# One hybrid mLSTM and attention encoder layer on one core: the seven-product weights on ScalarE's queue, their buffers in changing roles, and the merged projection's operands in six half-heads

## The chip, the core and the metric

The kernel runs on one core of a Trainium2 chip. Five engines work beside each other, each through its own list of instructions in order: PE (TensorE, matmul), DVE (VectorE), ACT (ScalarE), POOL (GpSimd) and SP (SyncE, which in this kernel issues the DMAs). The metric is the device time of one execution in microseconds. Three runs of the kernel before gave 1942.12, 1938.83 and 1942.77 us; their median is 1942.12 us.

## The reference

Two groups of 512 tokens go through the same layer with the same weights, all in 32-bit floating point. Cut to what matters here:

```python
h = rmsnorm(x, g_mix)
qk, v, o, gates, c_q, c_kv, k_r, gm = split(h @ w_in)
hm = mlstm(q, k, v, gates)                   # both directions, 4 heads of 256 columns
hm = rmsnorm(hm, g_mhead)
y_m = (sigmoid(o) * hm) @ w_mo               # 1024 x 1024
y_a = mla_attention(...) @ w_ao              # 8 heads of 128, w_ao 1024 x 1024
x = x + (sigmoid(gm_m) * y_m + sigmoid(gm_a) * y_a) @ w_out
h2 = rmsnorm(x, g_ffn)
x = x + (silu(h2 @ w_gate) * (h2 @ w_up)) @ w_down
x = x + sigmoid(x @ w_ple_gate) * (p @ w_ple)
return rmsnorm(x, g_final)
```

## The kernel before

**Products.** Every 32-bit product is made of three passes: an operand is split into a high part (`xh`, `whi`, written by a copy on ACT) and a low part (`xl`, `wlo`, written by a subtraction on DVE, `lo_of`), and high times high, low times high and high times low are added in PSUM. One pass is one MATMUL of 128x128 by 128x512. So each 128x512 tile that enters a matmul costs one ACT cast and one DVE subtraction.

**Seven products.** The large weight matrices (`w_mo`, `w_ao`, gate, up and down) are taken in 2x2 blocks, two row halves by the two token groups, with seven block products in place of eight. An object `Seven` holds one such 2x2 block of a weight: two 512 KB loads (`srcs[0]` with a11 and a12, `srcs[1]` with a21 and a22) go into two staging buffers `wst`, one from the pool WP and one from the pool WX. `weights(name)` gives the weights of one of the products P1, P2, P7, P6, P5, Q4, P3, in part by sums on POOL (`s3` for P7, then in place in a11, a21, a12), and `wsplit` splits them into a `wp` tile. P1, P2, P6 and P3 read the first buffer, P5 and Q4 the second, and P7 the sum `s3` of a11 and a21. The data operands of the seven products are held by an object `Ops`: from four tiles a, b, c, d for each k of four it makes the seven combinations (P1 = a, P2 = c, P7 = b - d, and so on, `part`), and `need` splits each.

**Chain.** `chain()` runs a list of `Seven`s with the products of neighbours interleaved (P6, next P1, P5, next P2, Q4, next P7, P3), and `outputs()` copies results from the PSUM bank b1 to a tile `u` on ACT and combines banks on DVE. The FFN's gate and up run as such `Seven`s from about 1186 us to 1586 us, its down from there to 1826 us, `w_mo` and `w_ao` from about 872 us to 1050 us.

**Attention.** From about 575 us to 872 us the loop over `hd` runs eight heads, each for two groups (sixteen half-heads). At head 7 it opens the pool X2, and there `hops.need` builds the data operands P1, P2 and P7 of the merged mLSTM projection (`w_mo`). `hraw` loads one tile of the mLSTM's result from `hzd` in DRAM and scales it in place by the per-row factors `hg` with an ACTIVATE. `hzd` is written by `mlstm_finish`, as (`to` + 1) times the transposed state.

**Order.** A scheduler lays the instructions of each engine in order from its own timeline model, except in sections between `pinned[0] = True` and `False`, whose order is the code's. The section around the embedding (`emb`) and the tail (from `finish(0, ...)` to the end) are pinned. All instructions of an engine pass through the wrapper `Engine` and carry the line of its call, L77; the DMAs carry their own lines (L849 the loads of `Seven`, L164 the other weights, L773 and L938 loads of activations, L982 the stores of z1d).

**Embedding and tail.** `emb` makes the products with `w_ple`, whose four splits are appended to `wple` when the first of their two columns comes up. At the end the last group is normalised in two halves of its tokens: `sums` adds squares over partitions by matmuls (`ssc`), `inv` makes the reciprocal root, `spread3` broadcasts it (`rbc`), and `finish` multiplies the output columns (`o`) and stores them.

Of the kernel before, what the change touches and what calls it, by code (L numbers as in the profile page):

```python
# [20 lines left out]
KD = D // P  # L21
# [41 lines left out]
def encoder_kernel(ctx: ExitStack, tc: tile.TileContext, a):  # L63
# [3 lines left out]
    class Engine:  # L67
# [5 lines left out]
        def __getattr__(self, name):  # L73
            f = getattr(self.e, name)

            def call(*args, **kw):
                r = f(*args, **kw)  # L77
                if pinned[0]:
                    tc.keep_in_program_order(r)
                return r  # L80

            return call

    V, S, E, GP = (Engine(e) for e in (nc.vector, nc.scalar, nc.tensor, nc.gpsimd))

# [376 lines left out]
    def mlstm_proj(hd):  # L462
# [59 lines left out]
        for c in range(2):  # L522
            w = w8(f"o{2 * hd + c}")
            for g in range(G):
                to[g][c] = hproj(w, g, M1("to", "to"))
                S.activation(out=to[g][c], in_=to[g][c], func=AF.Tanh, scale=0.5)
        mst[hd] = (sts, va, to)

    def mlstm_chain(hd, g):
# [67 lines left out]
        for c in range(2):  # L597
            tp = bank("ht")
            for i in range(NB):
                E.transpose(tp[:, i * P : (i + 1) * P], hm[:, i, c * P : (c + 1) * P], ident)  # L600
            zt = EV("ch", "hz")
            V.scalar_tensor_tensor(out=zt, in0=to[g][c], scalar=1.0, in1=tp, op0=ALU.add, op1=ALU.mult)
            nc.sync.dma_start(hzd[g][2 * hd + c], zt)
# [180 lines left out]
    class Ops:  # L784
# [12 lines left out]
        def part(self, name, k):  # L797
# [3 lines left out]
            if name == "P7":  # L801
                t = self.t[k] = self.tmp()
                add(out=t, in0=self.get("b", k), in1=self.get("d", k), op=ALU.subtract)
            elif name == "P6":
                t = self.t[k]
                add(out=t, in0=t, in1=self.get("a", k), op=ALU.subtract)
            elif name == "P5":
                t = self.get("a", k)
                add(out=t, in0=t, in1=self.get("b", k), op=ALU.subtract)
            else:  # L810
                t = self.t[k]
                add(out=t, in0=t, in1=self.get("c", k), op=ALU.add)
            return t
# [12 lines left out]
    wpn = [0]  # L826
# [14 lines left out]
    class Seven:  # L841


        def __init__(self, srcs, kh, ops, out):
            n = kh * P
            st = []
            for sl, src in zip((WP, WX), srcs):
                t = sl("wst", "wst", F32, (P, 1024))
                nc.sync.dma_start(t[:, : 2 * n], src)  # L849
                st += [t[:, 0:n], t[:, n : 2 * n]]  # L850
            self.st, self.n, self.kh, self.ops, self.out = st, n, kh, ops, out
            self.bk = {}
# [39 lines left out]
    def chain(quads, head=False, look=4):  # L892
# [10 lines left out]
        made = {}  # L903
        for at, (q, n) in enumerate(order):
            for i, m in order[at : at + look + 1]:
                quads[i][0].need(m)
            for i, m in order[at : at + 2]:
                if i not in made:
                    made[i] = quads[i][1]()
# [31 lines left out]

    def hraw(g, k):
        t = load(hzd[g][k], X2, "x")
        S.activation(out=t, in_=t, func=AF.Copy, scale=hg[:, k : k + 1])
        return t

    tmps = [(H, "rs"), (H, "rs"), (EV, "bk"), (EV, "bk")]
    hops = Ops(hraw, lambda: (lambda s: s[0](s[1], "t"))(tmps.pop(0)), lambda n: V if n == "P7" else GP)
# [5 lines left out]
    for hd in range(AH):  # L954
        if hd < AH - 1:
            wa = weight(a["wa"][hd + 1])
        else:
            QL.close()
            X2 = Slots("X2", "right", x=16)
            for n in ("P1", "P2", "P7"):  # L960
                hops.need(n)
        for g in range(G):
            attn(hd, g, ops[g])
            if hd < AH - 1:
                ops[g] = attn_proj(hd + 1, g, wa)
        for _ in range(BULK[2 + hd]):
# [109 lines left out]
    def emb(n):  # L1076
        for _ in range(n):
            c, g = todo.pop(0)
            if c // 2 == len(wple):
# [209 lines left out]
    finish(1, [0, 1, 2, 3], 0, H0)  # L1289
    embed(KD - 1, 1, bk[3], toks[1], bps[1])  # L1290
    sums(1, H0, H0)
    inv(1, H0)
    rs_ = rs2[1]
    spread3(1, H0, H0)
    rs2[1], rs_ = rs_, rs2[1]
    finish(1, [4, 5, 6, 7], 0, H0)
    rs2[1] = rs_
# [11 lines left out]
LEAD = 2  # L1309
LATN = (3, 0)  # L1310
# [94 lines left out]
```

## Time and profile before

| what | value |
|---|---|
| runs | 1942.12, 1938.83, 1942.77 us, median 1942.12 |
| profiled execution | 1939.74 us |
| its span, first to last instruction | 1938.0 us |
| mean granted PE clock | 0.981 |
| PE | 1861.9 us busy, x8836 |
| PE weight loads | 1542.6 us busy |
| DVE | 1260.3 us busy, x2135 |
| ACT | 874.7 us busy, x1711 |
| POOL | 474.4 us busy, x349 |
| DMA | 203.40 MB, mean 105 GB/s |

The profile shows one execution. Its time lies 2.38 us below the median of the runs, and 1.74 us of it lie outside the span. A busy PE means that a matmul is in flight; matmuls overlap (one lasts about 390 ns, and the next begins some 230 ns after it), so a short wait shows less idle time than it costs. In the views of stretches the columns are: the stretch and its length, then the busy time and number of instructions of PE, PE's weight loads, DVE, ACT and POOL, then the granted PE clock (1.00 is full), the DMA engines' busy share and the GB/s moved. In the chain of work that ended last each line is a start, a duration and what ran.

### The profile page before, as it was taken

The page shows a single profiled execution, that of the slowest core. Times are in us where ns is not written, and L with a number is a line of the kernel's source. Part 1 is how long each engine was busy: PE and PEld are TensorE (multiplying, and loading weights), DVE is VectorE, ACT ScalarE, POOL GpSimd, SP SyncE. Part 2 cuts the span into 40 slices and gives each one's busy share as a digit, 9 for nine tenths or more (in the row PEclk, how much of TensorE's full clock was granted, in tenths as well). Part 3 has the DMA queues.
Part 4 walks back from the last instruction along what each step waited for, and adds up shares of the span by engine and source line. Part 5 has one row for each costly group of instructions (what it writes and reads, how often), then busy time and mean ns, then how long its engine had stood idle before and what let it go on. Part 6 is the DMA issues. An engine that isn't in the chain of part 4 may idle for free. (4 is left out here: it accounts for less than half of the span.)

```text
span 1938.0 us, 24531 instructions
## 1 busy us (share of the span) xinstructions
PE 1861.9 (96%) x8836; PEld 1542.6 (80%) x8836; DVE 1260.3 (65%) x2135; ACT 874.7 (45%) x1711; POOL 474.4 (24%) x349
## 2 busy tenths in 40 slices
PE   7999999999999999979899989999999999999997
PEld 6888898988888888758777867777887777788886
DVE  7657575746455676878996667445444458778757
ACT  5245454535354566784533435233333344434442
POOL 3000000100000001234630014565466654232100
PEclk9999999999999999989999989999999999999998
DMA  4110112012262122137554331233223346534232
GB/s 161 50 44 33 55 35 64 34 60 82 82 202 90 55 74 73 53 115 239 163 200 153 109 114 66 87 111 106 94 97 102 115 135 218 163 120 142 87 125 87
DMA packets 95578, 203.40 MB, mean 105 GB/s; under 512 B 10400, under 2 KB 21024, under 8 KB 95456
## 3 DMA queue, kind: packets, MB, share of 16 engines
q1 hardware_dynamic: 95456, 201.83, 31.2%
q8 instruction: 69, 1.13, 0.2%
q14 instruction: 53, 0.43, 0.1%
HBM read 147.69 MB, written 54.10 MB: 104 GB/s over the span
## 5 line engine op out<-in xcount | busy, mean ns | idle before, releaser
L77 PE MATMUL b<-xh,wp 128*128 128x512 f32 x2296 | 723.4, 396 | 17.9 <-ACT wp L77 8.3
L77 PEld LDWEIGHTS b<-xh,wp 128*128 128x128 f32 x2296 | 434.5, 190 | 124.4 <-ACT wp L77 11.7
L77 PE MATMUL b<-xl,wp 128*128 128x512 f32 x1148 | 452.4, 394 | 5.9 <-DVE xl L77 5.7
L77 DVE TENSOR_TENSOR wp<-wst,wp 128x512 fp32r<-128x512 f32 (+1 forms) x284 | 271.9, 964 | 108.8 <-ACT wp L77 108.0
L77 ACT CAST wp<-wst 128x512 fp32r<-128x512 f32 (+1 forms) x284 | 171.0, 611 | 345.4 <-PE b L77 228.1
L77 PEld LDWEIGHTS b<-xl,wp 128*128 128x128 f32 x1148 | 217.8, 190 | 54.3 <-DVE xl L77 7.6
L77 PE MATMUL mm<-hh,whi 128*128 128x512 f32 x592 | 233.1, 394 | 7.2 <-ACT whi L77 7.0
L77 PE MATMUL mm<-hh,wlo 128*128 128x512 f32 x592 | 232.4, 394 | 2.2 <-DVE wlo L77 2.2
L77 PE MATMUL mm<-hl,whi 128*128 128x512 f32 x592 | 233.0, 394 | 1.1 <-DVE hl L77 1.1
L77 POOL TENSOR_TENSOR s<-wst,wst 128x512 f32<-128x512 f32 (+1 forms) x42 | 61.6, 1466 | 449.5 <-DMA wst<-w 323.4
L77 PEld LDWEIGHTS mm<-hh,whi 128*128 128x128 f32 x592 | 112.2, 190 | 30.6 <-ACT whi L77 7.0
L77 POOL TENSOR_TENSOR wst<-wst 128x512 f32<-128x512 f32 (+1 forms) x84 | 125.7, 1496 | 35.3 <-DVE wp L77 30.7
L77 PEld LDWEIGHTS mm<-hh,wlo 128*128 128x128 f32 x592 | 112.1, 189 | 26.1 <-DVE wlo L77 3.4
L77 PEld LDWEIGHTS mm<-hl,whi 128*128 128x128 f32 x592 | 112.1, 189 | 25.5 <-DVE hl L77 2.3
L77 DVE TENSOR_TENSOR u<-b,u 128x512 f32<-128x512 f32 x90 | 61.3, 687 | 107.6 <-PE b L77 82.7
L77 ACT CAST whi<-wst 128x1024 fp32r<-128x1024 f32 (+1 forms) x71 | 73.1, 1029 | 110.4 <-PE mm L77 77.6
L77 DVE TENSOR_TENSOR wlo<-wst,whi 128x1024 fp32r<-128x1024 f32 (+1 forms) x71 | 86.0, 1211 | 28.7 <-ACT whi L77 28.3
L77 POOL TENSOR_TENSOR vnl<-avt,vnh 128x512 fp32r<-128x512 f32 x16 | 21.5, 1345 | 317.6 <-ACT vnh L77 284.6
L77 DVE TENSOR_TENSOR xl<-ld,xh 128x512 fp32r<-128x512 f32 x109 | 88.7, 846 | 8.1 <-ACT xh L77 7.8
L77 PE MATMUL mm<-xh,wp 128*128 128x512 f32 (+1 forms) x288 | 81.7, 368 | 0.0
L77 ACT COPY u<-b 128x512 f32<-128x512 f32 x90 | 50.9, 586 | 66.6 <-PE b L77 65.6
L77 DVE TENSOR_TENSOR x<-x,b 128x512 f32<-128x512 f32 x84 | 56.9, 682 | 32.8 <-PE b L77 32.4
(269 smaller groups left out, 3379.4 us busy)
## 6 DMA issues: line engine op xcount, KB each, us to landing
wst<-w SPq DMA_DIRECT2D x135, 512.0 KB
ld<-actd SPq DMA_DIRECT2D x77, 256.0 KB
actd<-t SPq DMA_DIRECT2D x44, 256.0 KB
actd<-sg SPq DMA_DIRECT2D x33, 256.0 KB
x<-x SPq DMA_DIRECT2D x32, 256.0 KB
wst<-wd SPq DMA_DIRECT2D x16, 512.0 KB
hzd<-hz SPq DMA_DIRECT2D x16, 256.0 KB
tmd<-tg SPq DMA_DIRECT2D x16, 256.0 KB
```

The costliest lines, as they stand in the source:

```text
L77: r = f(*args, **kw)
```

## The change

1. `Seven` loads its weights with `S.dma_start`, so 84 loads leave SP's list and stand in ACT's. The pools of its two buffers change roles every two `Seven`s (`wsn`): the first load takes the pool WP in two of four, WX in the other two. The first buffer of a `Seven` thus follows the second buffer of the `Seven` two before, which is last read for Q4, and no longer that one's first buffer, which is last read for P3, the last product.
2. The operands P1, P2, P7 and P6 of the merged mLSTM projection are made in single (name, k) units behind the half-heads named in `HOPS`: three behind each half of heads 4 and 5, two behind each half of head 6. They load through four staging buffers. At head 7 the four tiles are loaded again into X2 for P5, Q4 and P3, so `hzd` is read 32 times (16 before, 256 KB each). Q4's operand is made of c - a - d by two POOL operations. The factor `hg` moves into `mlstm_proj`: an ACTIVATE (Identity, scale and bias `hc`) on `to` there, 16 in all, in place of the 16 scalings of the loads; `mlstm_finish` multiplies with `tensor_tensor`.
3. `emb` makes each `wple` split one ahead of its use.
4. In the tail `finish(1, ...)` of the first token half is split: two columns before the last `embed`, two behind it, two more between `inv` and `spread3`, two behind. The last `embed` runs with `keep=True`: it adds no squares on DVE, and `ssc` takes four more matmuls.
5. `Engine` gives back the plain method outside pinned sections. This changes only the line numbers in the profile: there instructions carry their own lines (L843 the cast and L152 the subtraction of a split, L855 the loads of `Seven`, L929 the copies to `u`).

The core of the diff:

```diff
                 S.activation(out=to[g][c], in_=to[g][c], func=AF.Tanh, scale=0.5)
+                hc = hg[:, 2 * hd + c : 2 * hd + c + 1]
+                S.activation(out=to[g][c], in_=to[g][c], func=AF.Identity, scale=hc, bias=hc)
...
-            V.scalar_tensor_tensor(out=zt, in0=to[g][c], scalar=1.0, in1=tp, op0=ALU.add, op1=ALU.mult)
+            V.tensor_tensor(out=zt, in0=to[g][c], in1=tp, op=ALU.mult)
...
-            else:
+            elif k in self.t:
                 t = self.t[k]
                 add(out=t, in0=t, in1=self.get("c", k), op=ALU.add)
+            else:
+                t = self.get("c", k)
+                add(out=t, in0=t, in1=self.get("a", k), op=ALU.subtract)
+                add(out=t, in0=t, in1=self.get("d", k), op=ALU.subtract)
...
-            for sl, src in zip((WP, WX), srcs):
+            for sl, src in zip((WP, WX) if wsn[0] % 4 < 2 else (WX, WP), srcs):
                 t = sl("wst", "wst", F32, (P, 1024))
-                nc.sync.dma_start(t[:, : 2 * n], src)
+                S.dma_start(t[:, : 2 * n], src)
                 st += [t[:, 0:n], t[:, n : 2 * n]]
+            wsn[0] += 1
...
+    stage = [(H, "rs"), (H, "rs"), (EV, "bk"), (EV, "bk")]
+    raws = [0]
+
     def hraw(g, k):
-        t = load(hzd[g][k], X2, "x")
-        S.activation(out=t, in_=t, func=AF.Copy, scale=hg[:, k : k + 1])
-        return t
...
+        raws[0] += 1
+        return load(hzd[g][k], *stage[raws[0] % 4])
...
+    units = [(n, [k]) for k in range(4) for n in ("P1", "P2", "P7", "P6")]
...
             X2 = Slots("X2", "right", x=16)
-            for n in ("P1", "P2", "P7"):
-                hops.need(n)
+            hops.r, hops.t = {}, {}
+            hops.raw = lambda g, k: load(hzd[g][k], X2, "x")
         for g in range(G):
             attn(hd, g, ops[g])
             if hd < AH - 1:
                 ops[g] = attn_proj(hd + 1, g, wa)
+            for _ in range(HOPS.get((hd, g), 0)):
+                hops.need(*units.pop(0))
...
-            if c // 2 == len(wple):
+            while len(wple) < min(4, c // 2 + 2):
...
-    finish(1, [0, 1, 2, 3], 0, H0)
-    embed(KD - 1, 1, bk[3], toks[1], bps[1])
+    first = rs2[1]
+    finish(1, [0, 1], 0, H0)
+    embed(KD - 1, 1, bk[3], toks[1], bps[1], True)
+    finish(1, [2, 3], 0, H0)
     sums(1, H0, H0)
     inv(1, H0)
-    rs_ = rs2[1]
+    finish(1, [4, 5], 0, H0)
     spread3(1, H0, H0)
...
-    finish(1, [4, 5, 6, 7], 0, H0)
+    finish(1, [6, 7], 0, H0)
...
+HOPS = {(4, 0): 3, (4, 1): 3, (5, 0): 3, (5, 1): 3, (6, 0): 2, (6, 1): 2}
```

**ACT in the FFN.** ACT's list at the change from one gate and up `Seven` to the next, before (`wp` are split weights, `s3` and `wst` their sources, `b1` a PSUM bank, `u` its copy):

```order
L77 CAST wp_2297_12504<-wst_2263_12313 128x512
L77 CAST wp_2302_12542<-wst_2263_12313 128x512
L77 CAST wp_2305_12563<-s3_2304_12560 128x512
L77 CAST wp_2307_12580<-wst_2262_12311 128x512
L77 COPY u_2293_12484<-b1_2267_12336 128x512
L77 COPY u_2296_12502<-b1_2295_12489 128x512
L77 CAST wp_2313_12619<-wst_2309_12597 128x512
L77 CAST wp_2311_12602<-wst_2290_12464 128x512
L77 COPY u_2298_12519<-b1_2267_12336 128x512
L77 CAST wp_2318_12656<-wst_2309_12597 128x512
```

The same place with the change (the `wst` tiles of the new loads are the first and the second buffer of the `Seven` after the next):

```order
L843 CAST wp_2309_12536<-wst_2275_12345 128x512
L843 CAST wp_2314_12574<-wst_2275_12345 128x512
L855 DMA wst_2321_12629<-w8 128x1024
L843 CAST wp_2317_12595<-s3_2316_12592 128x512
L843 CAST wp_2319_12612<-wst_2274_12343 128x512
L855 DMA wst_2322_12631<-w8 128x1024
L929 COPY u_2305_12516<-b1_2279_12368 128x512
L929 COPY u_2308_12534<-b1_2307_12521 128x512
L843 CAST wp_2325_12651<-wst_2321_12629 128x512
L843 CAST wp_2323_12634<-wst_2302_12496 128x512
L929 COPY u_2310_12551<-b1_2279_12368 128x512
L843 CAST wp_2330_12688<-wst_2321_12629 128x512
```

Two loads now stand in ACT's list behind the casts of Q4 and of P3 and ahead of the two copies to `u`. The first takes the buffer that Q4 has just read, the second the buffer that P3 has just read.

**DVE in the attention.** DVE's list beside the low part `qnl` of the queries for the second half of head 4, before (`wlo` is a low part of attention weights, `sc` are scores, `mx` their row values, `p` probabilities, `qnl` a low part of queries):

```order
L77 TENSOR_TENSOR qs1_1185_7163<-rp_1182_7154,qs1_1185_7163 64x512
L77 TENSOR_TENSOR wlo_1211_7328<-wst_1209_7324,whi_1210_7326 128x768
L77 TENSOR_REDUCE mx_1215_7338<-sc_1214_7332 128x1
L77 TENSOR_TENSOR qnl_1188_7177<-pj_1186_7168,qnh_1187_7175 128x512
L77 TENSOR_SCALAR mx_1215_7338<-mx_1215_7338 128x1
L77 TENSOR_REDUCE mx_1219_7358<-sc_1218_7352 128x1
L77 RECIPROCAL mx_1215_7338<-mx_1215_7338 128x1
L77 TENSOR_SCALAR mx_1219_7358<-mx_1219_7358 128x1
```

The same place with the change:

```order
L724 TENSOR_TENSOR qs1_1185_7179<-rp_1182_7170,qs1_1185_7179 64x512
L152 TENSOR_TENSOR xl_1243_7476<-ld_1241_7472,xh_1242_7474 128x512
L152 TENSOR_TENSOR wlo_1211_7344<-wst_1209_7340,whi_1210_7342 128x768
L748 TENSOR_REDUCE mx_1215_7354<-sc_1214_7348 128x1
L152 TENSOR_TENSOR xl_1246_7482<-ld_1244_7478,xh_1245_7480 128x512
L152 TENSOR_TENSOR qnl_1188_7193<-pj_1186_7184,qnh_1187_7191 128x512
L749 TENSOR_SCALAR mx_1215_7354<-mx_1215_7354 128x1
L748 TENSOR_REDUCE mx_1219_7374<-sc_1218_7368 128x1
L749 TENSOR_SCALAR mx_1219_7374<-mx_1219_7374 128x1
L752 RECIPROCAL mx_1215_7354<-mx_1215_7354 128x1
L805 TENSOR_TENSOR ld_1247_7484<-ld_1247_7484,ld_1248_7486 128x512
L752 RECIPROCAL mx_1219_7374<-mx_1219_7374 128x1
```

Two subtractions `xl` of the merged projection's operands P1 and P2 and the difference `ld` for P7 now stand between the attention's own instructions; the queries' `qnl` comes behind two of them.

**ACT at head 7.** ACT's list in the last half-head, before (`hg` are the row factors, `aph` high parts of transposed probabilities):

```order
L77 ACTIVATE ld_1420_8186<-ld_1420_8186,hg_81 128x512
L77 CAST xh_1406_8154<-ld_1405_8151 128x512
L77 ACTIVATE ld_1423_8193<-ld_1423_8193,hg_81 128x512
L77 ACTIVATE ld_1427_8201<-ld_1427_8201,hg_81 128x512
L77 ACTIVATE p_1470_8357,mx_1469_8354<-sc_1468_8348,mx_1469_8354 128x512
L77 ACTIVATE ld_1428_8204<-ld_1428_8204,hg_81 128x512
L77 ACTIVATE ld_1432_8213<-ld_1432_8213,hg_81 128x512
L77 ACTIVATE p_1462_8319<-p_1462_8319,mx_1461_8316 128x512
L77 ACTIVATE ld_1433_8216<-ld_1433_8216,hg_81 128x512
L77 ACTIVATE ld_1437_8225<-ld_1437_8225,hg_81 128x512
L77 ACTIVATE ld_1438_8228<-ld_1438_8228,hg_81 128x512
L77 CAST xh_1409_8161<-ld_1408_8158 128x512
```

And with the change (`vnh` is a high part of values, `oz` a copied output):

```order
L156 CAST vnh_1442_8242<-avt_1441_8240 128x512
L754 ACTIVATE p_1462_8315<-p_1462_8315,mx_1461_8312 128x512
L751 ACTIVATE p_1466_8335,mx_1465_8332<-sc_1464_8326,mx_1465_8332 128x512
L754 ACTIVATE p_1466_8335<-p_1466_8335,mx_1465_8332 128x512
L761 CAST aph_1450_8264<-pt_1455_8279 128x4x128
L770 COPY oz_1434_8215<-av_1433_8202 128x512
L761 CAST aph_1450_8264<-pt_1459_8299 128x4x128
L751 ACTIVATE p_1474_8373,mx_1473_8370<-sc_1472_8364,mx_1473_8370 128x512
L761 CAST aph_1450_8264<-pt_1463_8319 128x4x128
L754 ACTIVATE p_1474_8373<-p_1474_8373,mx_1473_8370 128x512
```

The scalings and the casts `xh` of P1 are gone from this place; what stands in these rows is the attention's own work.

More of the change, by code (lines that the diff above doesn't have):

```diff
@@ L74, in __getattr__ @@
             f = getattr(self.e, name)
+            if not pinned[0]:
+                return f
             def call(*args, **kw):
                 r = f(*args, **kw)
-                if pinned[0]:
-                    tc.keep_in_program_order(r)
+                tc.keep_in_program_order(r)
                 return r
@@ L801, in part @@
             if name == "P7":
-                t = self.t[k] = self.tmp()
+                t = self.t[k] = self.tmp() or self.get("b", k)
                 add(out=t, in0=self.get("b", k), in1=self.get("d", k), op=ALU.subtract)
@@ L824, in need @@
                     x.append((hi, lo))
-    wpn = [0]
+    wpn, wsn = [0], [0]
     def wpair():
@@ L903, in chain, with make @@
         made = {}
+        def make(i):
+            if i not in made:
+                made[i] = quads[i][1]()
         for at, (q, n) in enumerate(order):
@@ L906, in chain @@
                 quads[i][0].need(m)
-            for i, m in order[at : at + 2]:
-                if i not in made:
-                    made[i] = quads[i][1]()
+            for i, _ in order[at : at + 2]:
+                make(i)
             made[q].product(n)
@@ L939, in load4 @@
         return t
+    stage = [(H, "rs"), (H, "rs"), (EV, "bk"), (EV, "bk")]
+    raws = [0]
     def hraw(g, k):
-        t = load(hzd[g][k], X2, "x")
-        S.activation(out=t, in_=t, func=AF.Copy, scale=hg[:, k : k + 1])
-        return t
-    tmps = [(H, "rs"), (H, "rs"), (EV, "bk"), (EV, "bk")]
-    hops = Ops(hraw, lambda: (lambda s: s[0](s[1], "t"))(tmps.pop(0)), lambda n: V if n == "P7" else GP)
+        raws[0] += 1
+        return load(hzd[g][k], *stage[raws[0] % 4])
+    hops = Ops(hraw, None, lambda n: V if n == "P7" else GP)
+    hops.tmp = lambda: None
+    units = [(n, [k]) for k in range(4) for n in ("P1", "P2", "P7", "P6")]
     wa = weight(a["wa"][0])
@@ L1288, in encoder_kernel @@
     spread3(1, 0, H0)
-    finish(1, [0, 1, 2, 3], 0, H0)
-    embed(KD - 1, 1, bk[3], toks[1], bps[1])
+    first = rs2[1]
+    finish(1, [0, 1], 0, H0)
+    embed(KD - 1, 1, bk[3], toks[1], bps[1], True)
+    finish(1, [2, 3], 0, H0)
     sums(1, H0, H0)
     inv(1, H0)
-    rs_ = rs2[1]
+    finish(1, [4, 5], 0, H0)
     spread3(1, H0, H0)
-    rs2[1], rs_ = rs_, rs2[1]
-    finish(1, [4, 5, 6, 7], 0, H0)
-    rs2[1] = rs_
+    rs2[1], second = first, rs2[1]
+    finish(1, [6, 7], 0, H0)
+    rs2[1] = second
     finish(1, list(range(KD)), H0, H0)
```

## The prediction

> **What bounds the kernel now.** I read the page's busy times first, then its slices.
>
> ```profile
> PE 1861.9 (96%) x8836; PEld 1542.6 (80%) x8836; DVE 1260.3 (65%) x2135; ACT 874.7 (45%) x1711; POOL 474.4 (24%) x349
> PE   7999999999999999979899989999999999999997
> PEclk9999999999999999989999989999999999999998
> ```
>
> PE is in flight 96% of the span, and no other engine is over 65%. The change takes away no matmul of the large products (it adds four small `ssc`), so it can only win time in which PE stands still or runs at a lower clock. The slices show where that is: around the eighteenth, at 45% of the span, and in thin places behind it. The stretches and the waits of PE give their sizes.
>
> ```profile
> 750.00:795.40 45.40, 44.00 (x216) 35.56 (x215) 36.18 (x82) 34.40 (x72) 9.10 (x7) 1.00 0.21 69
> 795.40:838.00 42.60, 41.41 (x208) 34.26 (x207) 32.68 (x75) 33.68 (x71) 9.24 (x7) 1.00 0.31 105
> 838.00:872.00 34.00, 19.66 (x70) 13.95 (x69) 25.62 (x42) 27.65 (x54) 12.86 (x9) 0.75 0.20 71
> 1140.00:1150.00 10.00, 7.61 (x28) 5.55 (x26) 6.35 (x11) 4.48 (x9) 5.11 (x3) 0.85 0.42 154
> 1150.00:1160.00 10.00, 6.42 (x23) 4.63 (x22) 9.44 (x14) 4.88 (x10) 1.45 (x2) 0.84 0.33 116
> 1170.00:1180.00 10.00, 10.00 (x46) 8.22 (x45) 10.00 (x11) 4.15 (x8) 6.75 (x4) 1.00 0.01 2
> 1226.00:1240.00 14.00, 11.58 (x43) 8.77 (x42) 5.27 (x5) 3.39 (x6) 6.81 (x5) 0.88 0.25 76
> 1240.00:1586.00 346.00, 342.24 (x1481) 276.58 (x1480) 168.13 (x184) 118.44 (x210) 196.50 (x131) 1.00 0.31 102
> 1586.00:1592.00 6.00, 4.24 (x16) 2.81 (x15) 5.12 (x5) 3.38 (x6) 4.98 (x4) 0.90 0.96 337
> 1628.00:1645.00 17.00, 12.52 (x45) 9.54 (x44) 11.78 (x18) 7.46 (x13) 7.74 (x5) 0.80 0.86 310
> 1690.00:1702.00 12.00, 10.39 (x38) 7.82 (x37) 8.74 (x12) 4.62 (x9) 4.72 (x4) 0.86 0.45 147
> 1391.48 29.50 PE b L77 x128
> ```
>
> The last row, from the chain of work that ended last, gives PE's pace undisturbed: 29.50 us for 128 matmuls, 0.230 us each. A stretch's loss is its length less its matmuls at that pace. 838 to 872: 34.0 - 70 x 0.230 = 17.9 us. 1140 to 1160: 20.0 - 51 x 0.230 = 8.3. 1226 to 1240: 14.0 - 43 x 0.230 = 4.1. 1240 to 1586: 346.0 - 1481 x 0.230 = 5.4. 1586 to 1592: 2.3. 1628 to 1645: 6.7. 1690 to 1702: 3.3. Each includes the lower clock that follows a stop (0.75 to 0.90 in these rows).
>
> **Head 7, the largest loss.** In the window 826 to 873 ACT's and DVE's groups read:
>
> ```profile
> L77 ACT ACTIVATE ld<-ld,hg 128x512 f32<-128x512 f32 x16 | 11.5, 753 | 0.0
> L77 ACT CAST xh<-ld 128x512 fp32r<-128x512 f32 x10 | 6.0, 643 | 0.0
> L77 ACT CAST xh<-t 128x512 fp32r<-128x512 f32 x8 | 4.9, 620 | 5.2 <-POOL t L77 5.2
> L77 DVE TENSOR_TENSOR xl<-ld,xh 128x512 fp32r<-128x512 f32 x9 | 7.6, 855 | 2.6 <-ACT xh L77 2.5
> L77 DVE TENSOR_TENSOR t<-ld,ld 128x512 f32<-128x512 f32 x4 | 2.8, 692 | 1.0 <-ACT ld L77 1.0
> PE sc L77 <- ACT p L77: 9.8, 4, 3.6
> ```
>
> The 16 scalings (11.5 us) and 18 casts (10.9 us) are 22.4 us of ACT beside the softmax of the last half-heads, and the waits of PE (last row: total, times, longest) name ACT's `p`. The change takes both out of this place. The softmax's own chain stays; I leave it 3 us, under the longest such wait of 3.6. The gain here is 17.9 - 3 = 14.9 us.
>
> What it pays: 16 casts, 16 subtractions and 4 differences go into the half-heads of heads 4 to 6, by the new order nearly all beside what ran from 750 to 795 us. DVE gets 16 x 0.855 + 4 x 0.692 = 16.5 us where it was idle 45.4 - 36.18 = 9.2; ACT gets 16 x 0.643 = 10.3 where it was idle 11.0. All hidden costs 0, nothing hidden 16.5; what does not fit into DVE's idle time is 7.3, and since the following stretch has 9.9 idle on DVE I take 6. **Sum for the attention: -9** (-15 to +2). The 16 new ACTIVATEs on `to` and the changed multiplication stand in the mLSTM, where other work covers them:
>
> ```profile
> 100.00:430.00 330.00, 329.65 (x2014) 295.93 (x2012) 200.69 (x441) 164.21 (x403) 16.00 (x28) 1.00 0.14 47
> L77 POOL TENSOR_TENSOR t<-t,ld 128x512 f32<-128x512 f32 x11 | 19.8, 1818 | 4.9 <-DVE xl L77 4.9
> ```
>
> PE is never free in the mLSTM (first row) and ACT is at half; 16 x 0.753 = 12 us fit. If that cover is gone they cost up to 12; I take 0. The 16 repeated loads at head 7 (4.2 MB) run where the DMA share is 0.20 to 0.31, and nothing needs them before P5: 0. The last row is POOL from 872 to 985 us: Q4's four more operations come there at 1.8 us each, and P6's four leave it for the heads: 0, and up to 4 x 1.8 = 7 if they stand ahead of Q4 unhidden.
>
> **Weights of the seven products.** In that chain one stop per two `Seven`s looks like this (start, length, what):
>
> ```profile
> 1303.71 2.60 DVE wp L77 x2
> 1306.33 4.17 DMA wst<-w
> 1311.25 1.17 DVE wp L77
> 1312.46 13.12 PE b L77 x56
> 1629.18 3.59 DMA ld<-actd
> L77 PE MATMUL b<-xh,wp 128*128 128x512 f32 x987 | 308.1, 393 | 3.8 <-DVE wp L77 2.2 <-ACT u L77 1.6
> PE b L77 <- ACT wp L77: 7.5, 3, 4.5
> PE b L77 <- DVE wp L77: 4.9, 11, 1.7
> ```
>
> DVE finishes the split of P3, the last reader of the first buffer; then the load into it starts, lands 4.17 us later, is split, and PE goes on. With the roles changed the first load waits for Q4's split, which in the order stands ahead of `s3` and P3, so the chain from DVE through the DMA to P1 starts at least one split (1.3 us, half of the 2.60) and usually several microseconds earlier. The second `Seven`-load now comes after P3, but is first read for `s3` and P5, products later.
>
> From 1240 to 1586 that removes the waits for DVE's `wp`, 2.2 us in the group row and more with restarts, out of the 5.4 lost: -3, bounds 0 and -5.4. The three long waits for ACT's `wp` (7.5 us from 1186 to 1702) are the stops at 1226, 1586 and 1690, whose loss is 4.1 + 2.3 + 3.3 = 9.7 with some lower clock behind them: -10, bounds 0 and -12. At 1628 the load of an activation ends the chain, queued on SP behind others; SP loses 84 loads, so I take half of its 6.7: -3 (+2 to -6.7). **Sum: -16.**
>
> What ACT's new loads cost: on SP an issue takes 0.38 us, below.
>
> ```profile
> 902.64 0.38 SPq L849 DMA_DIRECT2D wst<-w  x1
> L77 ACT COPY u<-b 128x512 f32<-128x512 f32 x53 | 29.2, 586 | 19.4 <-PE b L77 18.6 <-POOL s L77 0.6
> ```
>
> 84 x 0.38 = 32 us on ACT, which in the FFN is busy 118.44 of 346 us. The issue itself is hidden; its wait is not surely so. ACT stands still until DVE has finished the split that the buffer waits for, with two copies to `u` behind it, and PE's bank b1 is free only after them. ACT now waits 18.6 us for PE ahead of 53 copies, so there is 0.35 us of slack on average. Bounds 0 and the 2.60 us of DVE at half of the changes; I take **+2**.
>
> In the Trainium skill, DMA: Bandwidth & Descriptors, section "Issuing engines are not separate DMA queues", loads issued by several engines run on the same 16 DMA engines and save only the issuing time; by it the move to ACT's queue is worth nothing and only the changed roles gain. The same page, "Anatomy of one DMA", puts a semaphore wait on the issuing sequencer; that speaks for the blocked queue, the last rival below.
>
> **Embedding and tail.** The prefetch of `wple` takes two of PE's stops from 1140 to 1160, but DVE is 9.44 and 10.00 us busy of ten in the rows of 1150 and 1170, and nothing is taken from DVE: of 8.3 us I take **-4** (0 to -8).
>
> ```profile
> 1923.00:1938.00 15.00, 2.57 (x12) 2.03 (x10) 9.51 (x30) 0.87 (x3) 0.00 (x0) 0.58 0.43 140
> 1931.98 2.74 DVE o L77 x7
> ```
>
> At the end DVE is the bound: seven outputs take 2.74 us, 0.39 each. Two move off the path, -0.8, and the squares of one column, -0.6, against four more `ssc`, +0.4: **-1** (+1 to -2).
>
> **Sum.** -9 - 16 + 2 - 4 - 1 = -28 against the profiled execution, 1938.0 us span and 1939.74 in all: 1911.7. That execution is 2.4 us under the median; I do not add this, since the changed kernel is compared by its own runs, and round down to **1911**.
>
> **The rivals.**
> 1. *The attention gives everything back.* DVE is the pacer of heads 4 to 6 when the 16.5 us come, nothing is hidden and `qnl` waits behind two `xl`: -15 + 16.5 = +2, so 1939.7 + 2 - 16 + 2 - 5 = 1923. For it: 9.2 us idle cannot take 16.5. Against: the idle time of the next stretch, and scheduled units that can slip.
> 2. *The next wait takes the place of the removed one.* The FFN's stops stay, since `s3` needs both buffers and the second is loaded later, or since PE there is held by the copies to `u`; the weights give -4 in place of -16: 1939.7 - 9 - 4 + 2 - 5 = 1924.
> 3. *The change does not do what it says:* the loads still start when they did, since the scheduler puts them behind other work in ACT's list, and head 7 is bound by its softmax alone (ACT's `p`): within 4 us of before, 1938.
> 4. *Slower: ACT's queue blocks.* At the end of each of the 42 `Seven`s ACT waits for DVE's split, the copies to `u` come late, and b1 holds PE. One block is at most 2.60 - 0.35 = 2.25 us; at half of the `Seven`s it costs 21 x 2.25 = 47 us: 1939.7 - 30 + 47 = 1957. It decides from a mean of 30 / 42 = 0.7 us for each `Seven`. For it: the order, two loads directly ahead of two copies. Against: PE waits for ACT's `u` are 1.6 us in 346 now, and DVE is at 49% there, so its split follows the cast closely.
>
> At 838 the granted clock is 0.75, and the loss above counts that in. In the Trainium skill, TensorE: Matmul & The Clock Gate, "Part 1: The HAM clock gate", an idle window of about 3.4 us halves PE's clock until it has been busy as long; the trace's lower clock directly behind the long stops agrees with it. By that page a spread of short waits in heads 4 to 6 would cost less than the one long stop.
>
> **How the numbers follow.** Forecast 0.62, rival 1 0.16, rival 2 0.10, rival 3 0.04, rival 4 0.08. The forecast's own range is 1893 (attention -15, embedding -8, weights -20, no cost on ACT) to 1922. The range takes in rivals 1 and 2 with their spread and ends at 1936, where rival 3 begins; 0.04 of better than all bounds is left out below 1893. A measurement of this kernel can tell about 0.2%, 3.9 us, from no change. Faster: 0.62 + 0.16 + 0.08 of rival 2 = 0.86, less 0.01 for the edge: 0.85. Same: 0.06. Slower: 0.09, rival 4 and a failed attention.
>
> **What would show it.** Right: from 838 to 872 the clock back near 1.00 and no group `ld<-ld,hg`; the waits for ACT's `wp` of 7.5 us gone; in the chain from 1240 on, runs of PE without a weight load between them; DVE over 42 us busy in the 45 at heads 4 to 6. Wrong: PE `b` waiting for ACT's `u` more than 10 us in all (rival 4), new waits for `qnl` or `mx` before 830 us (rival 1), or waits for POOL's `s3` in the FFN (rival 2).

## The result, and the profile after

The changed kernel takes 1912.59 us (median of 4 runs, 1909.99 to 1913.99), the kernel before 1942.44 us (4 runs). The ratio is 0.9848, with a 95% interval of 0.9831 to 0.9865. The forecast was 1911.0 us, with a range of 1893 to 1936. The profiled execution has a span of 1910.5 us, 27.5 less than before.

The page of the changed kernel, in the rows that answer to those shown of before:

```profile
PE 1845.7 (97%) x8840; PEld 1534.8 (80%) x8840; DVE 1240.0 (65%) x2134; ACT 878.6 (46%) x1711; POOL 474.4 (25%) x353
PE   7999999999999999899999988999999999999997
PEclk9999999999999999999999998999999999999999
```

PE is busy 16 us less, though it has four matmuls more. A matmul behind a stop lasts longer (0.79 us directly behind the stop that ends at 1633.99 us of the kernel before, against about 0.39) and counts as busy, so the time won is stops and the slow stretches behind them. The dent at 45% of the span has moved to 41% and become shallower; there is still one at 60%.

The waits of PE that bear on the change (total, times, longest):

```profile
PE b L894 <- ACT em L79: 10.2, 1, 10.2
PE b L895 <- DVE xl L152: 4.9, 1, 4.9
PE b L894 <- ACT u L929: 4.6, 9, 1.7
PE sc L742 <- ACT p L751: 3.1, 3, 1.3
PE pj L181 <- DVE mx L749: 2.9, 1, 2.9
```

ACT's `p` has gone from 9.8 to 3.1 us. Two waits are new: DVE's `mx` in the attention, at 763 us, and one long wait for ACT's copies `em` behind the embedding.

To place the gain I took the start of the same matmul in both traces: those into the banks b0 to b2 are 3444 in either kernel, counted here from the first of the chains. Differences of two starts give the length of a piece of the program, whatever came before it:

| piece, by matmul of the chains | before, us | after, us | difference | forecast |
|---|---|---|---|---|
| start to the first (gates, mLSTM, attention) | 871.36 | 862.73 | -8.6 | -9 |
| to the 504th (`w_mo`, `w_ao`) | 124.68 | 124.70 | 0.0 | 0 |
| to the 1008th (out, embedding, first FFN `Seven`s) | 254.00 | 246.64 | -7.4 | -4 - 4.1 |
| to the 2436th (gate and up) | 334.32 | 329.80 | -4.5 | -3 |
| to the 2520th (the stop at 1586) | 23.09 | 19.14 | -4.0 | -2.3 |
| to the 2688th (the stop at 1628) | 45.42 | 45.28 | -0.1 | -3 |
| to the 3024th (the stop at 1690) | 80.39 | 78.38 | -2.0 | -3.3 |
| to the last, 3443rd | 97.05 | 97.61 | +0.6 | 0 |
| last of these to the last matmul of all | 100.56 | 99.09 | -1.5 | -1 |

The differences sum to -27.5. In the row to the 1008th, -3.1 lie ahead of the 672nd matmul, in the embedding, and -4.6 between the 924th and the 1008th, at the stop of 1226.

The rows behind 1586 come from one execution each. Seven of the kernels below, the changed one among them, have the same order of work there on every engine. Their pieces at 1628 take 43.9 to 45.7 us, those at 1690 take 76.8 to 78.4 and the last ones 97.6 to 98.9. Three kernels have the order of before and take 45.3 to 45.7, 79.5 to 80.4 and 97.0 to 97.1. On the mean these three pieces change by -0.6, -2.5 and +1.1 us.

The chain of work that ended last shows the mechanism in gate and up. Its shares, before (1240 to 1586 us) and with the change (1200 to 1560):

```profile
by line: PE b L77 74.9%; DVE wp L77 9.5%; DMA wst<-w 9.4%; ACT wp L77 3.1%; DMA wst<-wd 1.2%; ACT u L77 1.0%; issue 0.7%; ACTq L77 0.2%
by line: PE b L894 33.4%; PE b L896 32.5%; PE b L895 32.4%; ACT u L929 1.0%; DVE wp L152 0.7%; issue 0.2%; ACT wp L843 0.2%; ACTq L929 0.0%; ACTq L843 0.0%
```

The weight loads have left that chain, and DVE's splits nearly so. The waits of PE from 1175 to 1680 us of the changed kernel show what went in the FFN:

```profile
PE b L894 <- ACT wp L843: 2.5, 1, 2.5
PE b L894 <- ACT u L929: 1.6, 6, 0.3
PE b L896 <- DVE wp L152: 0.7, 1, 0.7
```

Before, in the nearly matching window, ACT's `wp` was waited for 7.5 us in three stops, DVE's `wp` 4.9 in eleven. The stop of 2.5 us that is left is the one at 1628, now at 1605 us. The wait for `u` is unchanged, 1.6 in six.

### The profile page after: what moved, and what is told of

The parts are those of the page before. It is cut to its first block, busy times and chain, and to the rows that moved or that the text cites. A ratio compares the mean times of both kernels' runs of the same rounds, so it can differ in the third digit from the quotient of the medians.

```text
span 1910.5 us, 24510 instructions
## 1 busy us (share of the span) xinstructions
PE 1845.7 (97%) x8840; PEld 1534.8 (80%) x8840; DVE 1240.0 (65%) x2134; ACT 878.6 (46%) x1711; POOL 474.4 (25%) x353
## 3 DMA queue, kind: packets, MB, share of 16 engines
q8 instruction: 69, 1.13, 0.2%
## 4 chain that ended last, share of the span: by engine, by line
PE 83%; DVE 9%; issue 3%; ACT 2%; DMA 1%; POOL 1%; SPq 0%; ACTq 0%; DVEq 0%; POOLq 0%
PE b L894 12%; PE b L896 12%; PE b L895 12%; PE mm L181 8%; PE mm L183 8%; PE mm L182 8%; PE nm L580 3%; DVE xl L152 2%; PE mm L79 2%; PE mm L495 2%; PE mm L497 2%; PE mm L496 2%; DVE wp L152 1%; PE pt L759 1%; PE mm L1234 1%
## 5 line engine op out<-in xcount | busy, mean ns | idle before, releaser
L894 PE MATMUL b<-xh,wp 128*128 128x512 f32 x1148 | 444.1, 395 | 19.6 <-ACT em L79 10.2
L896 PE MATMUL b<-xh,wp 128*128 128x512 f32 x1148 | 446.3, 393 | 1.8 <-DVE wp L152 1.6
L843 ACT CAST wp<-wst 128x512 fp32r<-128x512 f32 (+1 forms) x271 | 164.4, 612 | 301.8 <-PE b L896 252.1
L152 DVE TENSOR_TENSOR wp<-wst,wp 128x512 fp32r<-128x512 f32 (+1 forms) x271 | 249.0, 921 | 78.2 <-ACT wp L843 78.0
L152 DVE TENSOR_TENSOR xl<-ld,xh 128x512 fp32r<-128x512 f32 x121 | 97.4, 836 | 10.1 <-ACT xh L827 5.0
L929 ACT COPY u<-b 128x512 f32<-128x512 f32 x90 | 50.9, 588 | 112.3 <-PE b L896 78.8
L152 DVE TENSOR_TENSOR wlo<-wst,whi 128x1024 fp32r<-128x1024 f32 (+1 forms) x70 | 86.4, 1234 | 24.6 <-ACT whi L166 24.4
L152 POOL TENSOR_TENSOR vnl<-avt,vnh 128x512 fp32r<-128x512 f32 x16 | 21.4, 1336 | 283.0 <-ACT vnh L156 260.3
```

The source lines that it names most:

```text
L152: e.tensor_tensor(out=out, in0=src, in1=hi.bitcast(F32), op=ALU.subtract)
L843: S.copy(hi, src)
L894: E.matmul(bk, whi[:, c], hi, start=bool(first) and k == 0, stop=False, **sk)
L896: E.matmul(bk, wlo[:, c], hi, start=False, stop=k == self.kh - 1, **sk)
```

## The experiments

Each kernel was profiled and timed beside the kernel before on the same chip. Single executions of an unchanged piece differ: in six kernels whose order of work on every engine is the same up to the chains, the piece from the 3901st matmul of the program (at 744 us) to the first of the chains took 118.2 to 120.9 us. So a difference under 3 us in that piece says nothing by itself; from the 1008th to the 2436th matmul the same six agree within 0.1 us.

**The two halves of the new weight loads.** First the queue alone, on the kernel before:

```diff
-                nc.sync.dma_start(t[:, : 2 * n], src)
+                S.dma_start(t[:, : 2 * n], src)
```

> The kernel before with one edit: the loads of Seven are issued from ACT, the two buffers keep their pools. Theory (the changed roles bring the gain in the FFN): the load of the next P1's weights still waits for the split of P3, so the stops stay; between the 924th matmul of the chains and the 2520th nothing over 3 us is won, time 1937 to 1946, and PE's waits for ACT's u grow over the 3.0 us of before. Rival (SP's list held the loads back): the stops at 1226 and 1586 us and those every two Sevens go, about 12 us won, time 1926 to 1932.

Then the roles alone, also on the kernel before, with the loads left on SP:

```diff
-            for sl, src in zip((WP, WX), srcs):
+            for sl, src in zip((WP, WX) if wsn[0] % 4 < 2 else (WX, WP), srcs):
```

> The kernel before with one edit: the buffers of Seven change roles every two Sevens, the loads stay on SP. Theory (roles): the load of the next P1's weights waits for Q4's split only; 10 to 14 us won between the 924th and the 2520th matmul of the chains, time 1926 to 1932. Rival (the queue is needed too): SP's list holds the early load behind stores that wait for POOL, under 6 us won, time 1935 to 1941.

Measured: the queue alone 1935.88 us, ratio 0.9979 (0.9964 to 0.9994); the roles alone 1929.69 us, 0.9941 (0.9919 to 0.9963). PE's waits from 1186 to 1702 us, with the queue alone:

```profile
PE b L77 <- DVE wp L77: 3.9, 5, 1.7
PE b L77 <- ACT wp L77: 3.6, 3, 2.0
```

and with the roles alone:

```profile
PE b L77 <- ACT wp L77: 5.9, 2, 5.1
PE b L77 <- DVE wp L77: 0.7, 1, 0.7
```

From the 1008th to the 2436th matmul the roles give -4.6, the same as the whole change, and -4.0 at 1586. Its wait of 5.1 us is the stop at 1628, which was 4.5 before. The queue alone gives -2.6 and -1.9 there. It loses 3.8 between the 672nd and the 756th matmul and wins 4.5 between the 924th and the 1008th: a stop came earlier. That shift need not come from the queue, since the kernel with the operands alone, whose loads stay on SP, shows it too (+2.6 and -2.6). So the theory held for the roles. For the queue it failed: nothing over 3 us was expected from the 924th to the 2520th matmul, and 9.0 were won there, 5.2 after what the shift took.

The opposite test leaves everything but the queue: the changed kernel with the loads back on SP.

```diff
-                S.dma_start(t[:, : 2 * n], src)
+                nc.sync.dma_start(t[:, : 2 * n], src)
```

> The changed kernel with the loads of Seven back on SP; the roles still change. Theory (the roles alone bring the FFN's gain; the queue matters only in heads 4 to 7, where the operands alone won 3.4 us and with the queue 8.6): from the 840th to the 2520th matmul of the chains within 1 us of the changed kernel, the first matmul of the chains 3 to 6 us later; time 1915 to 1919. Rival (the sum of parts differs for another reason): the first matmul within 1 us of the changed kernel, time 1911 to 1914.

Measured: 1913.94 us, ratio 0.9866 (0.9851 to 0.9881), which the intervals don't tell from the changed kernel's 0.9848. From the 840th to the 2520th matmul it differs from the changed kernel by 0.02 us. Once the roles change, the queue adds nothing in gate and up. Behind them it does bear on the stop at 1628, which is taken up below. The first matmul of the chains comes 3.4 us later; that is in the next group. In the Trainium skill, DMA: Bandwidth & Descriptors, "Issuing engines are not separate DMA queues", issuing from a further engine saves only issuing time; the 0.02 us agree with it in this stage.

**The attention.** The operands in half-heads without the rest of the change (old `Seven`, old embedding, old tail):

```diff
+            for _ in range(HOPS.get((hd, g), 0)):
+                hops.need(*units.pop(0))
```

> The changed kernel with the old Seven (SP, fixed roles), the old emb and the old tail: only the operands in six half-heads and the factor hg in the mLSTM are left of the change. Theory (head 7's burst of ACT was the loss, DVE in heads 4 to 6 the price): the first matmul of the chains begins 8 to 9 us earlier than before, the stretch of heads 4 to 6 is longer by some 8 us, and nothing else is won; time 1931 to 1936. Rival (the gain at that place came from the loads of the first Sevens): under 3 us, time 1937 to 1942.

Only the factor `hg` moved into the mLSTM, on the kernel before:

```diff
+                S.activation(out=to[g][c], in_=to[g][c], func=AF.Identity, scale=hc, bias=hc)
...
-        S.activation(out=t, in_=t, func=AF.Copy, scale=hg[:, k : k + 1])
```

> The kernel before with one edit: the factor hg is applied in the mLSTM, the operands are built at head 7 as before. Theory (ACT's 16 scalings and 18 casts share the loss at head 7): taking the 11.5 us of scalings alone away wins 5 to 9 us at the first matmul of the chains, and heads 4 to 6 pay nothing; time 1931 to 1937. Rival 1 (the spreading is what counts, the casts and subtractions hold the end): under 3 us won, time 1937 to 1942. Rival 2 (the scalings alone are the loss): over 12 us won, time under 1930, better than with the spreading.

The changed kernel without the spreading:

```diff
+            for n in ("P1", "P2", "P7"):
+                hops.need(n)
-HOPS = {(4, 0): 3, (4, 1): 3, (5, 0): 3, (5, 1): 3, (6, 0): 2, (6, 1): 2}
+HOPS = {}
```

> The changed kernel with the operands of the merged projection built at head 7 as before, with the factor hg still applied in the mLSTM. Theory (the scalings carry most of the loss at head 7, spreading adds little because DVE pays for it): heads 4 to 6 lose under 4 us and not 10.8, head 7 loses 14 to 17 and not 6.7; the first matmul of the chains comes 1 to 3 us later than in the changed kernel, time 1912 to 1917. Rival (spreading is the larger part): 6 to 9 us later, time 1918 to 1923.

And with half of the operands spread:

```diff
-    units = [(n, [k]) for k in range(4) for n in ("P1", "P2", "P7", "P6")]
+    units = [(n, [k]) for k in range(2) for n in ("P1", "P2", "P7", "P6")]
...
+            for n in ("P1", "P2", "P7"):
+                hops.need(n)
```

> The changed kernel with only the operands of k = 0 and 1 (8 of 16) in the half-heads and those of k = 2 and 3 at head 7. Theory (DVE's idle time of about 9 us in heads 4 to 6 holds half of the 16.5 us, the rest made PE wait): the loss from 750 to 800 us falls from 10.8 to 4 to 7 us, head 7 gives 2 to 4 of it back, the first matmul of the chains comes 1 to 5 us earlier than in the changed kernel; time 1905 to 1911. Rival (what is taken from DVE in heads 4 to 6 comes back at head 7): within 1 us, time 1911 to 1915.

Measured, with the length of three pieces, each over the same number of PE's matmuls (from the 3931st, the 4145th and the 4352nd of the program, at 750, 795 and 838 us of the kernel before, and to the first of the chains). Where the operands are spread, PE's order differs a little, so that two to six matmuls of over 60 in a piece are others:

| kernel | time, us | ratio (interval) | 750 to 795 | to 838 | to the chains |
|---|---|---|---|---|---|
| before | 1942.44 | 1 | 45.2 | 42.8 | 33.2 |
| changed | 1912.59 | 0.9848 (0.9831 to 0.9865) | 53.7 | 43.5 | 15.2 |
| operands alone | 1934.62 | 0.9966 (0.9949 to 0.9982) | 56.0 | 44.9 | 16.6 |
| changed, loads on SP | 1913.94 | 0.9866 (0.9851 to 0.9881) | 54.9 | 46.8 | 15.2 |
| factor alone | 1936.02 | 0.9977 (0.9965 to 0.9989) | 45.1 | 42.8 | 26.7 |
| changed, not spread | 1916.01 | 0.9867 (0.9851 to 0.9884) | 45.1 | 42.8 | 26.6 |
| changed, half spread | 1920.96 | 0.9896 (0.9881 to 0.9910) | 50.1 | 42.8 | 28.0 |

Taking the 16 scalings off ACT wins 6.5 us at head 7 and costs nothing elsewhere. Spreading wins another 11.4 there and pays 9.2 before. The 2.2 that are left lie under the 3 us by which executions of this piece differ, and the two kernels' intervals overlap, so a net gain of the spreading isn't shown. The operands alone were expected to bring the chains 8 to 9 us earlier and brought 3.4. The stretches of the changed kernel show who takes the payment:

```profile
750.00:795.40 45.40, 39.54 (x189) 31.40 (x188) 41.64 (x81) 35.88 (x73) 13.52 (x10) 1.00 0.52 164
795.40:838.00 42.60, 40.28 (x196) 32.16 (x195) 35.22 (x82) 33.60 (x70) 7.77 (x6) 1.00 0.15 47
838.00:862.00 24.00, 20.81 (x104) 15.72 (x103) 15.62 (x35) 17.68 (x36) 17.92 (x14) 1.00 0.67 240
```

DVE is busy 41.6 of 45.4 us where it had 36.2, PE 39.5 where it had 44.0. PE's new waits up to 838 us are for DVE's `mx` (2.9 us) and `qnl` (1.7, before 0.4). Behind 838 the clock is back at 1.00 and ACT, 27.65 of 34 before, has room. With the loads on SP the order that the scheduler makes of DVE's work in heads 4 to 6 is another one, and the spreading then pays 13.0 and 13.7 us there, more than it wins. Half of the spreading was the worst: it pays 4.9 in the first piece and wins nothing at head 7 over the kernel without spreading, against the expectation. There PE waits for DVE's low parts `apl` and hardly for ACT (stretch of the half-spread kernel, and PE's largest wait in it):

```profile
838.00:870.00 32.00, 23.70 (x89) 17.84 (x88) 24.57 (x39) 18.22 (x38) 20.82 (x14) 0.74 0.47 152
PE pt L759 <- DVE apl L152: 5.7, 2, 3.0
```

**The embedding.** The changed kernel with the old splits of `wple`:

```diff
-            while len(wple) < min(4, c // 2 + 2):
+            if c // 2 == len(wple):
```

> The changed kernel without the early splits of wple. Theory (the early splits win what their section shows, the stops of PE between 1100 and 1200 us become one): 2 to 4 us later at the 672nd matmul of the chains and the wait for em under 4 us, with waits for wp in its place; time 1914 to 1917. Rival (DVE ends the section in either case): within 1 us, time 1911 to 1914.

Measured: 1921.74 us, ratio 0.9910 (0.9894 to 0.9926); counted from the 504th matmul of the chains it is 2.6 us later than the changed kernel at the 672nd and 6.7 at the 756th. The second part was not expected. ACT's timeline there (start, length, idle time before it and what ended it):

```profile
1176.42 0.62 ACT L843 CAST wp<-wst 128x512 fp32r<-128x512 f32 x1
1177.79 0.34 ACTq L855 DMA_DIRECT2D wst<-w  x1
1178.17 0.62 ACT L843 CAST wp<-s 128x512 fp32r<-128x512 f32 x1 [1.13 <-DVE wp L152]
1180.96 0.33 ACTq L855 DMA_DIRECT2D wst<-w  x1
1181.34 0.59 ACT L929 COPY u<-b 128x512 f32<-128x512 f32 x1 [2.03 <-DVE wp L152]
```

The cast of P7's weights, for which PE waits 4.5 us until 1178.84, stands behind a load that waits for DVE's split of Q4. That is the blocked queue of rival 4, but it holds the cast only 1.13 us, and PE doesn't wait for the copy to `u` that the second load holds. The chain of work that ended last comes to this place from POOL, through ACT's own list (the row at 1174.12 is a table load of ACT):

```profile
1153.78 8.49 POOL s L869
1174.12 1.28 ACT L1135
1178.17 0.63 ACT wp L843
```

From the 504th to the 1008th matmul the pieces are 254.0 us before, 250.3 with the roles alone on SP, 253.3 in this kernel and 246.6 in the changed one. So the roles' gain of 3.7 there isn't seen in this kernel; of that loss about 1.1 us is traced to the queue, and the rest stays open.

The wait of 10.2 us for `em` looked like ACT's order, since the copies stand behind casts that wait for DVE. Two kernels moved them:

```diff
         emb(1)
-        h2.need("P7", [k])
         emb(1)
+        h2.need("P7", [k])
```

> The changed kernel, but in the embedding's section both products of a step stand ahead of the split of P7's operand, so that ACT copies them out of PSUM before it waits for DVE. Theory (the one wait of 10.2 us for ACT's copies em is a matter of ACT's order): it falls under 5 us and PE begins the FFN earlier, 2 to 5 us won; time 1907 to 1911. Rival (DVE ends that section, whatever ACT does): a wait for DVE's xl of the same size takes its place, within 1.5 us of the changed kernel.

```diff
+    emb(len(todo))
     for k in range(4):
         h2.get("b", k)
         h2.get("d", k)
-        emb(1)
         h2.need("P7", [k])
-        emb(1)
-    emb(len(todo))
```

> The changed kernel, but all sixteen products of the embedding stand ahead of the four splits of P7's operands. Theory (the wait for em is ACT's order, and the run with pairs ahead left the last two copies behind the last split): the wait for em goes under 2 us, PE begins the FFN 5 to 9 us earlier, DVE's splits become late in part; 3 to 7 us won, time 1906 to 1910. Rival (DVE ends that section): waits for DVE's xl of 6 us or more follow within the next 30 us, nothing won, time 1911 to 1914.

Measured: with pairs ahead 1912.64 us, ratio 0.9850 (0.9835 to 0.9864), the wait still 8.6 us. With all ahead 1920.13 us, 0.9898 (0.9884 to 0.9913): the wait for `em` is gone and, counted from the 504th matmul, PE reaches the 672nd, the first of the FFN, 8.9 us earlier, yet the 756th 5.9 us later; that is slower than either expectation. Its waits of PE from 1155 to 1190 us, and its stretches:

```profile
PE b L896 <- DVE wp L152: 2.8, 2, 1.5
PE b L894 <- ACT wp L843: 2.6, 1, 2.6
PE b L895 <- DVE xl L79: 2.5, 1, 2.5
PE b L894 <- ACT xh L79: 1.7, 1, 1.7
PE b L895 <- DVE xl L152: 1.6, 1, 1.6
```

```profile
1148.00:1160.00 12.00, 12.00 (x54) 9.87 (x53) 9.98 (x16) 4.44 (x8) 1.57 (x2) 1.00 0.14 49
1160.00:1170.00 10.00, 4.27 (x14) 2.42 (x12) 10.00 (x18) 6.74 (x13) 3.04 (x1) 0.80 0.00 0
1170.00:1180.00 10.00, 5.32 (x12) 3.15 (x12) 10.00 (x10) 6.60 (x11) 7.48 (x5) 0.67 0.15 52
1180.00:1190.00 10.00, 9.25 (x29) 7.34 (x30) 5.47 (x7) 2.83 (x5) 3.04 (x3) 0.68 0.24 79
```

and the same place of the changed kernel:

```profile
1140.00:1160.00 20.00, 9.75 (x36) 7.61 (x35) 19.96 (x27) 12.40 (x25) 8.35 (x5) 0.74 0.29 110
```

DVE is full in both. The wait for `em` was cover for DVE's splits. Without it PE runs into them one by one, several short stops in a row, at a clock of 0.67 to 0.80 for 30 us. The stops add up to about what the one long wait took. The difference is in the clock: in the changed kernel much of the low clock falls into the wait itself (0.66 from 1144.5 to 1154.5 us, with no matmul in flight). Behind it PE runs 3.5 us at 0.52 and has 1.00 again from 1158 us.

If DVE ends the section, less DVE work in it should help. All four splits first, ahead of the stretch in which DVE is full:

```diff
-            while len(wple) < min(4, c // 2 + 2):
+            while len(wple) < 4:
```

> The changed kernel with all four splits of wple made before the embedding's first product. Theory (DVE ends the embedding's section, and two splits fewer in its full stretch from 1128 to 1165 us shorten it by what they take there, 0.7 to 1.5 us each): the wait for em falls from 10.2 to 7 to 9 us, PE begins the FFN 1.4 to 3 us earlier and keeps it; time 1909 to 1912. Rival (the splits hold the section's start instead, ahead of sums and the broadcast of the root): within 0.5 us or later than the changed kernel, time 1912 to 1915.

```profile
PE b L894 <- ACT em L79: 7.1, 1, 7.1
```

Measured: 1913.56 us (1906.10 to 1914.15), ratio 0.9850 (0.9832 to 0.9869). The wait falls to 7.1 us, but the piece from the 504th to the 756th matmul is only 0.6 us shorter; the splits hold its start instead, since its first product comes 135.4 us behind the 504th matmul, against 132.9 in the changed kernel and about 134.5 in the two that moved the copies. No version beats the changed kernel beyond its interval.

**The stop at 1628.** The changed kernel with the down projection's activations loaded from ACT:

```diff
-                    src = load(actd[self.f0 + j, name], OP, "ev")
+                    src = OP("ev", "ld")
+                    S.dma_start(src, actd[self.f0 + j, name])
```

> The changed kernel with the activation loads of the down projection issued from ACT. Theory (the loads stood in SP's list behind stores that wait for POOL, so fewer loads on SP changed nothing): the waits at 1603 to 1611 us (7.0 us lost between 1600 and 1650) shrink to under 4; time 1908 to 1911. Rival (the loads wait for their buffers, which the last sums of POOL hold): ACT now stands in that wait with casts behind it, the loss stays or grows by 2 to 6 us; time 1912 to 1919.

In the chain of work that ended last before, the load that PE waits for stands behind POOL's sum and the store of it:

```profile
1625.72 1.63 POOL t L77
1627.37 0.32 SPq L1134
1629.18 3.59 DMA ld<-actd
```

In the changed kernel SP's list and POOL's read there:

```profile
1599.85 3.28 SPq L1150 DMA_DIRECT2D actd<-t  x3
1603.22 0.88 SPq L775 DMA_DIRECT2D ld<-actd  x2
```

```profile
1601.15 1.63 POOL L1146 TENSOR_TENSOR t<-t,sg 128x512 f32<-128x512 f32 x1
```

The load goes out directly behind the third store, which waited for POOL's sum until 1602.78. With the loads on ACT the time is 1917.37 us, ratio 0.9877 (0.9863 to 0.9892), and the stop is longer by 1.8 us (47.1 us from the 2520th to the 2688th matmul). ACT's list shows why:

```profile
1604.64 0.34 ACTq L855 DMA_DIRECT2D wst<-wd  x1
1605.02 0.62 ACT L843 CAST wp<-wst 128x512 fp32r<-128x512 f32 x1 [6.34 <-DVE wp L152]
1608.05 0.34 ACTq L855 DMA_DIRECT2D wst<-wd  x1
1608.42 4.93 ACTq L1168 DMA_DIRECT2D ld<-actd  x6
```

The activation's load now stands behind two weight loads that wait for DVE. Of the 5.0 us by which this execution is longer than the changed kernel's, 1.8 lie here; 2.8 lie ahead of the 672nd matmul, before the place of the edit. Whether on SP the stores alone held the load, or also its own buffer, this does not settle; that stays open.

The stop itself did become shorter with the change: PE waits 2.2 to 2.9 us for ACT's `wp` in the seven kernels with this order, and 4.5 to 5.4 us in the five with the weight loads on SP (4.5 before, 5.1 with the changed kernel's loads back on SP). So the queue brought it; by which step of the chain isn't traced. The piece didn't follow, and the granted clock shows why. The stop and what is behind it, before:

```profile
1629.50:1634.00 4.50, 0.02 (x2) 0.01 (x1) 2.50 (x4) 2.44 (x5) 0.00 (x0) 0.75 1.03 363
1634.00:1638.60 4.60, 4.60 (x10) 3.36 (x11) 4.60 (x9) 3.60 (x7) 0.87 (x1) 0.50 1.04 396
```

and in the changed kernel:

```profile
1605.40:1607.80 2.40, 0.00 (x0) 0.00 (x0) 0.50 (x1) 1.15 (x3) 0.00 (x0) 1.00 0.98 344
1607.80:1615.20 7.40, 6.69 (x16) 4.70 (x17) 7.40 (x10) 5.33 (x10) 4.50 (x3) 0.54 0.91 338
```

Before, a part of the low clock fell into the stop, and PE ran at 0.50 for 4.6 us. Now all of it falls on work, 7.4 us at 0.54 with a second short stop, and that takes up most of the 2.0 us won at the stop.

## Why the prediction was right

The time, the sign and the mechanism of the largest terms were right. That the sum of -28 meets the -27.5 of the traces so closely is luck: single terms are off by up to 3 us, in both directions, and runs of the changed kernel differ by 4 us. By its own steps:

- **Attention, -9:** measured -8.6. Both terms under it were too small: head 7 won 18.0 us (33.2 to 15.2) where 14.9 were forecast, since the 3 us left for the softmax's chain were not needed, and the payment in heads 4 to 6 was 9.1 (8.4 and 0.7) where 6 were. The cause is split by the runs: 6.5 us are the scalings, and the spreading gives back most of what it wins, with a net gain that isn't shown. The sum gave the queue no part here; it has one, by the order of DVE's work.
- **Weights, -16:** the roles do it, as argued from the two buffers' last readers. Gate and up -4.5, and -4.0 at 1586, are more than forecast. At 1586 the stretch that was counted ends at 1592, and the low clock behind that stop does not (0.72 from 1592 to 1596 us). 1690 gave -2.0, not -3.3. One reading was wrong: the three waits for ACT's `wp`, 7.5 us, are not the stops at 1226, 1586 and 1690 but those at 1231 (1.9), 1634 (4.5) and 1695 (1.1); at 1590 PE waits 1.7 us for DVE's `wp`. The sum goes by the losses of the stretches, so no term changes by this; but these waits could not all go with the roles, since the longest is the stop at 1628, and 2.5 us of it are left. The term that failed is that stop's: "SP loses 84 loads, so I take half of its 6.7". The piece gained 0.1 (0.6 on the mean). The stop did fall from 4.5 to 2.5 us, but PE then ran longer at the low clock, which the halved loss left out; and what is left of the stop is a load behind stores that wait for POOL, as it was before.
- **ACT's loads, +2:** in gate and up nothing (0.02 us between the queues), so the copies to `u` are not late where DVE has room. Without the early splits of `wple` the blocked queue holds one cast for 1.1 us.
- **Embedding, -4:** together with the stop at 1226 (-4.1) forecast -8.1, measured -7.4. The embedding's own part is -3.1, the stop's -4.6, which the roles alone also give. Five short stops, 6.2 us in sum, became one wait of 10.2 us. PE stands still longer, but less of its work runs at the low clock, much of which falls into the wait now. The bound by DVE was right.
- **Tail, -1:** measured -1.5. The nine kernels with the new tail take 99.1 us there, the five with the old one 100.2 to 100.6. The waits at the end agree with the argument, DVE's outputs end the kernel in both.

The last outputs in the chain of work that ended last in the changed kernel:

```profile
1897.62 0.78 DVE o L79 x2
1902.44 1.65 DVE o L79 x4
1904.47 2.74 DVE o L79 x7
```

The seven outputs at the end take the same 2.74 us as before; of the two groups of four ahead of them, one (1.57 us before) has become two outputs.

- **Rivals 1 and 2** did not come: the attention's payment is real but half of the gain, and no wait for POOL's `s3` appears in the FFN. Rival 1's sign did show, new waits for `mx` and `qnl` before 830 us, and DVE was 41.6 us busy at heads 4 to 6 where over 42 were called right. So its mechanism is there, at 9.1 us and not 16.5. Rival 3 is excluded by the pieces. Rival 4 shows once, with 1.1 us; PE's waits for `u` are 4.6 us in all, under the 10 of its sign.
- That short waits would cost less than one long stop agrees with heads 4 to 6 (granted clock 1.00 in both stretches of the changed kernel) and not with the kernel that had all `em` ahead: there short stops close together held the clock at 0.67 to 0.80, and cost more than the long one. The prediction took its rule from the Trainium skill, TensorE: Matmul & The Clock Gate, "Part 1: The HAM clock gate", an idle window of about 3.4 us. The trace of before shows the low clock behind shorter stops too: 0.72 behind the 1.7 us that end at 1590, and 0.86 from 1690 to 1702 with stops of 1.1 and 0.5 us. In the changed kernel 2.9 us of standing still at 763 us lowered nothing (1.00 from 750 to 795). The length of one stop doesn't decide it here; what does stays open.

## What to carry to other kernels

When two staging buffers take turns, look at which reader releases each, and give the buffer that is free first to the load that is wanted first; in gate and up that was worth more (4.6 us) than another queue to issue from (2.6). Work that is taken off a full engine has to be paid where it goes: add up the idle time of the receiving engine, and expect the waits there to cost about the overflow and more. A single long wait may be the cover of an engine that is full beneath it, and taking the wait away then uncovers many short ones. When a stop is shortened, look at the clock behind it before the difference is counted as won.

## What the runs showed that was not expected

- The order that the scheduler makes of DVE's work in heads 4 to 6 depends on the queue of other loads, though nothing in the attention's code differs. It moved the attention by about 4 us: from the 3901st matmul to the chains 123.0 and 123.7 us with the loads on SP, 118.2 to 120.9 with them on ACT.
- Removing half of a burst won nothing there: 28.0 us at head 7 with half of the operands, 26.6 with all of them, and the kernel with half took 1920.96 us against 1916.01.
- At the stop of 1628 executions with the same order of work differ by 1.8 us, with stops of nearly one length. In the clock records the low clock behind it lasts 3.41 us in the three shortest pieces (43.9 to 44.5) and 6.83 in the four others (45.2 to 45.7).
- A DMA issued from ACT shows as an instruction of 0.33 us in ACT's list, and the next instruction carries its wait: 6.34 us idle ahead of one cast in the kernel with the activation loads on ACT.
